# Strassen products that accumulate onto a PSUM bank of an earlier product

## The chip, the cores and the metric

The kernel runs on one core of one Trainium2 chip. The metric is the device time of one execution in microseconds (us); three runs of the kernel before gave 1822.58, 1822.8 and 1824.99 us, median 1822.8.

## The reference

One layer of a Griffin-style block on x (1024 tokens, 1024 channels), float32 in and out. Cut to what matters here:

```
mod = silu(c) @ ada_w + ada_b                # sh1, sc1, g1, sh2, sc2, g2
h = rmsnorm(x, ln1_g) * (1 + sc1) + sh1
q, k, v, cb, cc, cx, ga, gb = split(h @ w_in)
y_a = stick_breaking_attention(norm(q), norm(k), v)
y_b = cb * causal_dwconv(cc * cx, conv_w)
merged = sigmoid(ga) * (y_a @ w_branch_a) + sigmoid(gb) * (y_b @ w_branch_b)
x = x + g1 * (merged @ w_out)
h = rmsnorm(x, ln2_g) * (1 + sc2) + sh2
f = (silu(h @ w_ffn_gate) * (h @ w_ffn_up)) @ w_ffn_down
x = x + g2 * f
```

The FFN has 2816 hidden channels. Two stages are touched: the columns of `w_in` that give cb, cc, cx, ga and gb (called the gates below), and the FFN's gate and up projections.

## The kernel before, in words

A float32 matrix is held as a high part (float32r) and a low part, and a product of two matrices is three matmuls: high with high, high with low, low with high. TensorE (PE) works on 128x512 tiles; a product of the two-level scheme below takes 12 matmuls (`half_prod`, L126 to L133: four slices of the contraction, three matmuls each, on lines L131, L132 and L133). Weights come by DMA as `raw` (SyncE's queue), ScalarE (ACT) makes the high part `whi`, VectorE (DVE) the low part `wlo`.

The gates and the FFN's gate and up projections use Strassen's scheme in Winograd's form. A block computes four 128x512 outputs, c11, c12, c21, c22, from seven products P1 to P7 (the factor in the code counts from 0, so P6 is factor 5). The weight sums S1 to S4 are made by GpSimd (POOL) from the raw halves, in `ws` tiles; the sums of the activations (the factors `ft`, `rh`/`rl`, `big`) exist already. There are 20 such blocks in the gates (`for g, (sec, j) in enumerate(gates)`, L730) and 22 in the FFN (`strassen(j, e, ...)`, j from 0 to 10, e = 0 for gate, 1 for up). With every product in a PSUM bank of its own, a block ends in one copy on ScalarE and seven sums on VectorE (helper `tt`, L136):

```
c11 = P1 + P2
c21 = P1 + P6;  c12 = c21 + P5;  c22 = c12 + P7
c21 = c21 + P7;  c21 = c21 + P4;  c12 = c12 + P3
```

The gates have six banks (`pj`), the FFN eight (`e`).

What follows a block: in the gates a sigmoid (L749) and a store issued on ScalarE's queue (L750), or the short convolution (L721 to L724). Between the blocks stands other work: `mods_later`, which makes the later modulation vectors from `ada_w`. It loads 512 KB pieces (`ad<-ada`, `uu<-ada`, issued on ScalarE's queue, L639), takes a dot on VectorE over 128x1024 elements (L640), turns the sums by two transposes (`tr`), copies them (`uu`, L655) and stores a vector (`d_g<-uu`, L656). In the FFN a Silu (L1453) or a product with the gate side follows, then the seven operands that the down projection needs of the hidden values (four of them sums, on POOL, for the first and last j on VectorE), each split and stored by `put_f` (ScalarE L1445, VectorE L1446 through L136, store L1447). c11 of the gate side lives in the tile `wt(0)`, which these hidden sums read.

The start of the FFN is written out by hand: while the last token tiles of x are normalised (`tail_tr`, `tail_ev`, transposes L1206), the activation's quarters `h2b` are combined and split by `split_big` (ScalarE L1199 into `rh` and `big`, VectorE into `rl`), and the first products P1 and P2 of (0, gate), (0, up), (1, gate) and (1, up) are made ahead into `pre` and `pq`.

The order within an engine is set by a tile scheduler that walks the program with its own cost table; every engine then works its list strictly in order, and waits at semaphores for others. An instruction that waits therefore holds all that stand behind it in its engine's list, DMA issues on ScalarE's and SyncE's lists included.

Of the kernel before, what the change touches and what calls it, by code (L numbers as in the profile page):

```python
# [12 lines left out]
ALU = mybir.AluOpType  # L13
# [17 lines left out]
def block_kernel(tc, x, x_t, cols, ada_1, ada_2, ada_row, w_q, w_kv, w_cg, w_a, w_b, w_o, w_g, w_u, w_d, out):  # L31
# [91 lines left out]
        nc.gpsimd.tensor_tensor(out=r, in0=m[:, :w], in1=nhalf[:, :w], op=ALU.pow)  # L123
        return r

    def half_prod(ps, w, fh, fl):  # L126

        wh = w[0].rearrange("p (k m) -> p k m", k=4)
        wl = w[1].rearrange("p (k m) -> p k m", k=4)
        for k in range(4):  # L130
            nc.tensor.matmul(ps, wh[:, k, :], fh[:, k, :], start=(k == 0), stop=False)  # L131
            nc.tensor.matmul(ps, wh[:, k, :], fl[:, k, :], start=False, stop=False)  # L132
            nc.tensor.matmul(ps, wl[:, k, :], fh[:, k, :], start=False, stop=(k == 3))  # L133

    def tt(eng, out, a, b, op):
        eng.tensor_tensor(out=out, in0=a, in1=b, op=op)  # L136
# [375 lines left out]
    def g_split(src):  # L512
        split_at.append(split_at.pop(0))
        hi, lo = (split_at[0].tile([P, 512], F32R, tag=t_, bufs=GS if split_at[0] is gw else GS2, name=nm(t_))
                  for t_ in ("whi", "wlo"))
        nc.scalar.activation(hi, src, AF.Copy)
        tt(nc.vector, lo, src, hi.bitcast(F32), ALU.subtract)
        return hi, lo
# [75 lines left out]
    def g_prod(w, q):  # L594
        ps = g_bank()
        half_prod(ps, w, *fac[q])
        return ps
# [132 lines left out]
    for g, (sec, j) in enumerate(gates):  # L730
        raw, raw2 = raws
        p1, p2 = pre[g] if g in pre else (g_prod(g_split(raw[:, :512]), 0), g_prod(g_split(raw[:, 512:]), 1))
        a11, a12, a21, a22 = raw[:, :512], raw[:, 512:], raw2[:, :512], raw2[:, 512:]
        s1, s2_, s3, s4 = (gp2.tile([P, 512], F32, tag=f"ws{q}", bufs=1, name=nm("ws")) for q in range(4))
        with tc.high_priority() if g == 0 else ExitStack():
            tt(nc.gpsimd, s3, a11, a21, ALU.subtract)
            tt(nc.gpsimd, s2_, a22, s3, ALU.subtract)
            w6 = g_split(s2_)
        tt(nc.gpsimd, s1, a21, a22, ALU.add)
        ws4 = nc.gpsimd.tensor_tensor(out=s4, in0=a12, in1=s2_, op=ALU.subtract)  # L740
        if g + 1 < len(gates):
            raws = two_raw(g + 1)
        c11, c21, c12, c22 = (gp.tile([P, 512], F32, tag=f"c{q}", bufs=2, name=nm("c")) for q in range(4))

        def put(c, m, n):
            if sec == 5:
                pend.append((c, m, n))
            elif sec > 2:
                nc.scalar.activation(c, c, AF.Sigmoid)  # L749
                nc.scalar.dma_start((d_sga, d_sgb)[sec - 3][m, :, n * 512:(n + 1) * 512], c)  # L750
            elif sec == 1:
                ccs[m, n] = c
            elif n == 1 and m >= 4:
                ccs["late"] = c
            else:
                put_u(c, m, n)
                if n == 0 and m >= 4:
                    put_u(ccs["late"], m, 1)

        def later():  # L760
            if len(pmm) > 1 or pmm and not pend:
                sum_q(*pmm.pop(0))
            if pend:
                put_q(*pend.pop(0))
            elif g > 3 and not pmm:
                with tc.issue_after(ws4.ins):
                    next(eq, None)

        nc.scalar.activation(c11, p1, AF.Copy)
# [462 lines left out]
    NJ = NH // 2  # L1232
    pq = {}

    def prod(ps, w, q):
        half_prod(ps, w, rh[q], rl[q])

    def product(w, q):
        ps = bank()
# [137 lines left out]
    tt(nc.vector, x1p, pq[6], x1p, ALU.add)  # L1377
# [27 lines left out]
    def strassen(j, e, src, done=lambda q, c: None):  # L1405

        c21, c12, c22 = (ct(f"c{q}{e}", 1) for q in range(1, 4))
        if (j, e) == (0, 0):
            tt(nc.vector, c12, pq[5], x1p, ALU.add)
            p4 = product(sp5, 3)  # L1410
            tt(nc.vector, c22, pq[7], c12, ALU.add)
            tt(nc.vector, c21, pq[7], x1p, ALU.add)
            tt(nc.vector, c12, pq[3], c12, ALU.add)
            tt(nc.vector, c21, p4, c21, ALU.add)
            return x11, c12, c21, c22
        p1, p2, s1, s2, s3, s4, a22 = wsum(j, e, src, nc.gpsimd)
        if (j, e) == (0, 1):
            c11, c1 = x21, x2p
        else:
            c11, c1 = ct("c01", 1) if e else wt(0), c21  # L1420
            nc.scalar.activation(c21, p1, AF.Copy)  # L1421
# [5 lines left out]
        p5 = product(split(s1), 4)  # L1427
        tt(nc.vector, c12, p5, c21, ALU.add)
        p7 = product(split(s3), 6)
        tt(nc.vector, c22, p7, c12, ALU.add)  # L1430
        done(3, c22)
        tt(nc.vector, c21, p7, c21, ALU.add)
        p3 = product(split(s4), 2)
        tt(nc.vector, c12, p3, c12, ALU.add)
        done(1, c12)
        p4 = product(split(a22), 3)
        tt(nc.vector, c21, p4, c21, ALU.add)
        done(2, c21)
        return c11, c12, c21, c22

# [252 lines left out]
```

## Time and profile before

| | |
|---|---|
| median of 3 runs | 1822.8 us (1822.58 to 1824.99) |
| the profiled execution, its span | 1822.9 us |
| PE busy | 1794.7 us, 98% |
| VectorE busy | 1362.9 us, 75% |
| ScalarE busy | 809.6 us, 44% |
| GpSimd busy | 367.4 us, 20% |
| chain that ended last | PE 83%, VectorE 8%, DMA 5%, ScalarE 1% |

The kernel before stands for 1822.8 us; the trace shows one execution, whose span of 1822.9 us is that time. A matmul's row lasts 0.39 us, but matmuls overlap, so time on PE is counted from start to start. A row of the view of waits reads: engine, the output and line that waited, what released it, then the total in us, how often, and the longest. In square brackets a row of the timeline shows the idle time ahead of it and what ended it.

### The profile page before, as it was taken

What the parts mean: (1) busy time and instruction counts of PE and PEld (TensorE: products, weight loads), DVE (VectorE), ACT (ScalarE), POOL (GpSimd) and SP (SyncE); (2) the same over time, 40 slices, a digit from 0 to 9 for tenths busy, and PEclk for the clock granted to TensorE, in tenths of its full rate; (3) what the DMA queues carried; (4) which work ended last, traced back from release to release, by engine and by line L of the source; (5) the groups of instructions that cost most, each with busy time, mean ns of one, the idle gap of its engine ahead of it and who ended that gap; (6) DMA issues with size and microseconds to landing.
All of it is one profiled execution on the core that took longest, in us unless ns stands there. A gap on an engine that the chain in (4) does not pass through costs nothing.

```text
span 1822.9 us, 24550 instructions
## 1 busy us (share of the span) xinstructions
PE 1794.7 (98%) x8629; PEld 1492.0 (82%) x8629; DVE 1362.9 (75%) x1980; ACT 809.6 (44%) x1510; POOL 367.4 (20%) x277
## 2 busy tenths in 40 slices
PE   8999999999999899999999999999999999999999
PEld 6888877888778788888888888877888888878887
DVE  5876586778894699999997554699877878644776
ACT  5534363333433466666675221764444344322321
POOL 0024234632232000000000000115434444200000
PEclk9999999999999999999999999999999999999999
DMA  9479644223684977696654546424443444299876
GB/s 381 162 247 386 235 163 141 81 98 125 230 287 155 265 203 185 191 336 172 160 135 153 184 155 204 129 91 183 164 150 139 150 169 155 107 347 346 274 230 220
DMA packets 165102, 359.57 MB, mean 197 GB/s; under 512 B 15522, under 2 KB 60906, under 8 KB 163828
## 3 DMA queue, kind: packets, MB, share of 16 engines
q1 hardware_dynamic: 128300, 289.65, 48.6%
q10 hardware_dynamic: 35672, 64.68, 9.9%
q0 software_dynamic: 1008, 3.67, 0.5%
q8 instruction: 69, 1.13, 0.3%
q14 instruction: 53, 0.43, 0.1%
HBM read 247.32 MB, written 110.66 MB: 196 GB/s over the span
## 4 chain that ended last, share of the span: by engine, by line
PE 83%; DVE 8%; DMA 5%; issue 2%; ACT 1%; POOL 0%; SPq 0%; ACTq 0%; DVEq 0%; POOLq 0%
PE e L131 7%; PE e L133 7%; PE e L132 7%; PE pj L293 7%; PE pj L131 5%; PE pj L133 5%; PE pj L132 5%; PE pj L995 4%; PE pj L997 4%; PE pj L996 4%; PE e L1521 4%; PE e L1523 4%; PE e L1522 4%; PE tr L919 3%; PE o L935 2%
## 5 line engine op out<-in xcount | busy, mean ns | idle before, releaser
L905 DVE TENSOR_TENSOR_SCAN pt<-pt,mk 128x128 f32<-128x128 f32 (+7 forms) x128 | 172.6, 1348 | 3.2 <-ACT pt L897 3.2
L131 PE MATMUL e<-big,whi 128*128 128x512 f32 x352 | 138.2, 393 | 3.8 <-ACT c L1421 3.8
L132 PE MATMUL e<-big,whi 128*128 128x512 f32 x352 | 137.9, 392 | 0.0
L133 PE MATMUL e<-big,wlo 128*128 128x512 f32 x352 | 137.8, 392 | 0.0
L293 PE MATMUL pj<-whi,big 128*128 128x512 f32 x448 | 133.7, 396 | 3.1 <-ACT big L262 3.1
L136 DVE TENSOR_TENSOR c<-e,c 128x512 f32<-128x512 f32 x138 | 92.9, 687 | 54.8 <-PE e L133 53.8
L131 PE MATMUL pj<-big,whi 128*128 128x512 f32 x320 | 125.3, 392 | 1.6 <-DVE c L136 1.6
L133 PE MATMUL pj<-big,wlo 128*128 128x512 f32 x320 | 124.9, 390 | 0.0
L132 PE MATMUL pj<-big,whi 128*128 128x512 f32 x320 | 124.6, 389 | 0.0
L122 POOL TENSOR_SCALAR rs_m<-ss 128x1 f32<-128x1 f32 x8 | 1.7, 218 | 607.5 <-ACT xn L1324 607.5
L1521 PE MATMUL e<-whi,f 128*128 128x512 f32 (+1 forms) x319 | 121.8, 382 | 0.9 <-ACT whi L1182 0.6
L1522 PE MATMUL e<-wlo,f 128*128 128x512 f32 (+1 forms) x319 | 121.8, 382 | 0.0
L1523 PE MATMUL e<-whi,f 128*128 128x512 f32 (+1 forms) x319 | 121.6, 382 | 0.0
L136 DVE TENSOR_TENSOR c<-pj,c 128x512 f32<-128x512 f32 x140 | 93.1, 682 | 36.0 <-PE pj L133 35.2
L897 ACT ACTIVATE pt<-z,rq 128x512 f32<-128x512 f32 (+1 forms) x192 | 105.1, 576 | 25.4 <-PE z L896 25.0
L995 PE MATMUL pj<-big,whi 128*128 128x512 f32 x256 | 113.9, 445 | 0.0
L136 POOL TENSOR_TENSOR ws<-raw,raw 128x512 f32<-128x512 f32 x40 | 54.1, 1354 | 278.3 <-DMA raw<-w_cg 130.0
L923 DVE TENSOR_TENSOR atl<-tr,ath 128x512 fp32r<-128x512 f32 (+1 forms) x192 | 103.1, 550 | 9.2 <-ACT ath L922 7.2
L922 ACT ACTIVATE ath<-tr 128x512 fp32r<-128x512 f32 (+1 forms) x192 | 93.2, 488 | 33.1 <-PE tr L919 32.2
L132 PE MATMUL e<-rl,whi 128*128 128x512 f32 x264 | 102.8, 390 | 1.5 <-DVE rl L136 1.5
L133 PE MATMUL e<-rh,wlo 128*128 128x512 f32 x264 | 102.7, 389 | 0.0
L131 PE MATMUL e<-rh,whi 128*128 128x512 f32 x264 | 102.7, 389 | 0.0
(269 smaller groups left out, 4863.2 us busy)
## 6 DMA issues: line engine op xcount, KB each, us to landing
f<-d_f SPq DMA_DIRECT2D x77, 512.0 KB, 4.3
d_f<-fs SPq DMA_DIRECT2D x70, 512.0 KB, 3.2
raw<-w_cg SPq DMA_DIRECT2D x40, 512.0 KB, 3.2
raw<-w_u SPq DMA_DIRECT2D x26, 512.0 KB, 3.3
raw<-w_g SPq DMA_DIRECT2D x25, 512.0 KB, 3.6
raw<-w_kv SPq DMA_DIRECT2D x20, 512.0 KB, 4.0
ad<-ada ACTq DMA_DIRECT2D x19, 512.0 KB, 4.5
ld<-ada SPq DMA_DIRECT2D x16, 512.0 KB, 4.3
```

The lines of the kernel that those rows point to most:

```text
L131: nc.tensor.matmul(ps, wh[:, k, :], fh[:, k, :], start=(k == 0), stop=False)
L132: nc.tensor.matmul(ps, wh[:, k, :], fl[:, k, :], start=False, stop=False)
L133: nc.tensor.matmul(ps, wl[:, k, :], fh[:, k, :], start=False, stop=(k == 3))
L136: eng.tensor_tensor(out=out, in0=a, in1=b, op=op)
L293: nc.tensor.matmul(ps, a, b, start=(k == 0 and q == 0), stop=(k == KT - 1 and q == 2))
L897: nc.scalar.activation(pt[:, off + s0:off + s0 + m], z[:, :m], AF.Sigmoid, scale=rq[:, 1, i, h:h + 1])
L905: nc.vector.tensor_tensor_scan(out=pt[:, rev], data0=pt[:, rev], data1=mk[:, rev], initial=1.0, op0=ALU.mult, op1=ALU.max)
L923: nc.vector.tensor_tensor(out=tl[:, :nb, c0:c0 + P], in0=src, in1=th[:, :nb, c0:c0 + P].bitcast(F32), op=ALU.subtract)
L995: nc.tensor.matmul(ps, wh, rh_, start=(k == 0), stop=False)
L1521: nc.tensor.matmul(o, sh, w[0][:, c], start=(j == 0), stop=False)
L1522: nc.tensor.matmul(o, sh, w[1][:, c], start=False, stop=False)
L1523: nc.tensor.matmul(o, sl, w[0][:, c], start=False, stop=(j == NJ - 1))
```

## The change

In a block, P6 and then P5 are accumulated onto P1's bank, and P4 onto P7's bank, by matmuls whose first one does not clear the bank. ScalarE copies P1's bank three times: as c11 (P1), after P6 as c21 (P1+P6), after P5 as c12 (P1+P6+P5). VectorE is left with four sums: c11 + P2, c12 + P7 (into c22), c12 + P3, and c21 + P7, which by then holds P7+P4. P6 may start when c11's copy has read the bank, P5 when c21's has, P4 when c22's sum has read P7's bank. In the gates' first block P4 keeps a bank of its own. At the FFN's start the up side's P6 and P5 are interleaved with the gate side's, and its P7 is made there too.

```diff
-    def half_prod(ps, w, fh, fl):
+    def half_prod(ps, w, fh, fl, onto=False):
...
-            nc.tensor.matmul(ps, wh[:, k, :], fh[:, k, :], start=(k == 0), stop=False)
+            nc.tensor.matmul(ps, wh[:, k, :], fh[:, k, :], start=(k == 0 and not onto), stop=False, skip_group_check=onto)
...
+        def onto(ps, src, q):
+            half_prod(ps, src if isinstance(src, tuple) else g_split(src), *fac[q], onto=True)
+
         nc.scalar.activation(c11, p1, AF.Copy)
-        p4 = g_prod(g_split(a22), 3) if g + 1 == len(gates) else None
-        p6 = g_prod(w6, 5)
-        tt(nc.vector, c21, p6, c11, ALU.add)
+        onto(p1, w6, 5)
         tt(nc.vector, c11, p2, c11, ALU.add)
         put(c11, j, 0)
         later()
-        p5 = g_prod(g_split(s1), 4)
-        tt(nc.vector, c12, p5, c21, ALU.add)
-        p3 = g_prod(g_split(s4), 2) if g == 0 else None
-        p7 = g_prod(g_split(s3), 6)
+        p7, p3 = (None, g_prod(g_split(s4), 2)) if g == 0 else (g_prod(g_split(s3), 6), None)
+        nc.scalar.activation(c21, p1, AF.Copy)
+        onto(p1, s1, 4)
+        nc.scalar.activation(c12, p1, AF.Copy)
+        p7 = p7 or g_prod(g_split(s3), 6)
         tt(nc.vector, c22, p7, c12, ALU.add)
         put(c22, j + 4, 1)
         later()
-        tt(nc.vector, c21, p7, c21, ALU.add)
         p3 = p3 or g_prod(g_split(s4), 2)
         tt(nc.vector, c12, p3, c12, ALU.add)
         put(c12, j, 1)
         later()
-        p4 = p4 or g_prod(g_split(a22), 3)
-        tt(nc.vector, c21, p4, c21, ALU.add)
+        if g:
+            onto(p7, a22, 3)
+        else:
+            tt(nc.vector, c21, p7, c21, ALU.add)
+            p7 = g_prod(g_split(a22), 3)
+        tt(nc.vector, c21, p7, c21, ALU.add)
...
-    pq[6] = product(sp2, 5)
-    pq[5] = product(sp1, 4)
-    pq[3] = product(sp3, 2)
+    up2 = split(ws1[1])
+    prod(pq[1], sp2, 5, True)
+    prod(pre[0, 1][0], up2, 5, True)
+    nc.scalar.activation(x1p, pq[1], AF.Copy)
+    up1 = split(ws1[0])
+    prod(pq[1], sp1, 4, True)
+    nc.scalar.activation(x2p, pre[0, 1][0], AF.Copy)
+    x14 = wsb(0)
+    nc.scalar.activation(x14, pq[1], AF.Copy)
...
     split_big(rh[6], rl[6], h2b[0][0])
+    pq[3] = product(sp3, 2)
+    prod(pre[0, 1][0], up1, 4, True)
     pq[7] = product(sp4, 6)
...
         if (j, e) == (0, 1):
-            c11, c1 = x21, x2p
+            c11, c21, p1, p7 = x21, x2p, pre[0, 1][0], pq["up"]
         else:
-            c11, c1 = ct("c01", 1) if e else wt(0), c21
+            c11 = ct("c01", 1) if e else wt(0)
+            nc.scalar.activation(c11, p1, AF.Copy)
+            prod(p1, split(s2), 5, True)
+            tt(nc.vector, c11, p2, c11, ALU.add)
+            p7 = product(split(s3), 6)
             nc.scalar.activation(c21, p1, AF.Copy)
-            tt(nc.vector, c11, p2, c21, ALU.add)
-        p6 = bank()
-        prod(p6, split(s2), 5)
-        tt(nc.vector, c21, p6, c1, ALU.add)
+            prod(p1, split(s1), 4, True)
+        nc.scalar.activation(c12, p1, AF.Copy)
```

The lists of PE keep their number of matmuls; VectorE's goes from 1947 to 1822 rows, ScalarE's from 1610 to 1694. Lines below L770 stand some 5 to 10 lines further down in the new kernel. Three places of ScalarE's list follow.

In the gates, ScalarE's list from the store of the first later modulation vector (`d_g0`) on; L639 are loads of `ada_w` pieces, L769 is the copy of a block's P1. Before:

```order
L656 DMA d_g0_80<-uu_824_4307 128x1024
L639 DMA ad_904_4665<-ada_2 128x1024
L516 ACTIVATE whi_872_4519<-raw_844_4380 128x512
L639 DMA ad_937_4822<-ada_2 128x1024
L769 ACTIVATE c_846_4384<-pj_834_4338 128x512
L639 DMA ad_939_4827<-ada_2 128x1024
L639 DMA uu_863_4485<-ada_2 128x1024
```

The same place in the new list; L772 is the copy of P1 (c11), L780 the copy that gives c12:

```order
L656 DMA d_g0_80<-uu_780_4249 128x1024
L639 DMA ad_854_4599<-ada_2 128x1024
L639 DMA ad_884_4752<-ada_2 128x1024
L639 DMA ad_886_4757<-ada_2 128x1024
L780 ACTIVATE c_768_4154<-pj_754_4106 128x512
L516 ACTIVATE whi_806_4346<-ws_796_4312 128x512
L639 DMA uu_816_4423<-ada_2 128x1024
L772 ACTIVATE c_802_4326<-pj_790_4280 128x512
```

The load `uu_816` waits for the store of `d_g0`; a copy of P1 now stands right behind it, where before the next copy of P1 stood ahead of the loads of `uu`.

At the FFN's start, ScalarE's list around the split of the activation sums (`rh6` and `rh3`, L1199). Before:

```order
L1199 ACTIVATE big_2374_11682<-h2b11_11069 128x1024 x2
L1369 ACTIVATE wt_2380_11756<-e_2355_11612 128x512
L1199 ACTIVATE big_2374_11682<-h2b01_11068 128x1024 x2
L1199 ACTIVATE rh6_11684<-h2b00_11070 128x1024 x2
L1182 ACTIVATE whi_2387_11825<-raw_2386_11823 128x512
L1182 ACTIVATE whi_2400_11951<-ws_2208_10753 128x512
```

The same place in the new list, where `split_big` is L1204; L1380, L1383 and L1385 are the copies of the two P1 banks after P6 and after P5:

```order
L1374 ACTIVATE wt_2321_11678<-e_2296_11534 128x512
L1204 ACTIVATE big_2315_11604<-h2b01_10990 128x1024 x2
L1187 ACTIVATE whi_2323_11686<-ws_2149_10675 128x512
L1380 ACTIVATE wt_2302_11568<-e_2276_11452 128x512
L1187 ACTIVATE whi_2325_11715<-ws_2148_10674 128x512
L1383 ACTIVATE wt_2321_11678<-e_2296_11534 128x512
L1385 ACTIVATE ws_2327_11732<-e_2276_11452 128x512
L1204 ACTIVATE rh6_11606<-h2b00_10992 128x1024 x2
```

Three copies of accumulated banks and two splits now stand ahead of `rh6`.

In the middle of the FFN, ScalarE's list where a block's copy of P1 follows the copies `fs` of the hidden sums of the block before. Before:

```order
L1445 ACTIVATE fs_2689_13291<-wt_2685_13278 128x512
L1445 ACTIVATE fs_2693_13314<-c10_2624_12995 128x512
L1445 ACTIVATE fs_2694_13319<-wt_2686_13279 128x512
L1182 ACTIVATE whi_2746_13545<-ws_2737_13511 128x512
L1421 ACTIVATE c10_2695_13323<-e_2703_13336 128x512
```

The same place in the new list:

```order
L1187 ACTIVATE whi_2651_13400<-ws_2647_13391 128x512
L1454 ACTIVATE fs_2602_13175<-wt_2598_13162 128x512
L1454 ACTIVATE fs_2605_13197<-c10_2542_12886 128x512
L1432 ACTIVATE wt_2622_13255<-e_2615_13219 128x512
L1187 ACTIVATE whi_2653_13417<-ws_2648_13392 128x512
```

The copy of P1 goes into the tile `wt` instead of a tile of c21, and P6 of the same block is in PE's list behind it, 43 matmuls after P1's last.

More of the change, by code (lines that the diff above doesn't have):

```diff
@@ L130, in half_prod @@
         for k in range(4):
-            nc.tensor.matmul(ps, wh[:, k, :], fh[:, k, :], start=(k == 0), stop=False)
-            nc.tensor.matmul(ps, wh[:, k, :], fl[:, k, :], start=False, stop=False)
-            nc.tensor.matmul(ps, wl[:, k, :], fh[:, k, :], start=False, stop=(k == 3))
+            nc.tensor.matmul(ps, wh[:, k, :], fh[:, k, :], start=(k == 0 and not onto), stop=False, skip_group_check=onto)
+            nc.tensor.matmul(ps, wh[:, k, :], fl[:, k, :], start=False, stop=False, skip_group_check=onto)
+            nc.tensor.matmul(ps, wl[:, k, :], fh[:, k, :], start=False, stop=(k == 3), skip_group_check=onto)
     def tt(eng, out, a, b, op):
@@ L1408, in strassen @@
         if (j, e) == (0, 0):
-            tt(nc.vector, c12, pq[5], x1p, ALU.add)
-            p4 = product(sp5, 3)
-            tt(nc.vector, c22, pq[7], c12, ALU.add)
+            tt(nc.vector, c22, pq[7], x14, ALU.add)
+            tt(nc.vector, c12, pq[3], x14, ALU.add)
+            pq["up"] = product(split(ws1[2]), 6)
+            prod(pq[7], sp5, 3, True)
             tt(nc.vector, c21, pq[7], x1p, ALU.add)
-            tt(nc.vector, c12, pq[3], c12, ALU.add)
-            tt(nc.vector, c21, p4, c21, ALU.add)
             return x11, c12, c21, c22
```

15 lines of the change are left out of this document (5 added, 10 removed).

## The prediction

> **What bounds the kernel now.** I read the page's busy shares first, then the waits of TensorE, then windows of 20 us over the two touched stages (gates about 190 to 590 us, FFN gate/up about 1190 to 1590 us), then the timeline at each lost stretch.
>
> ```profile
> PE 1794.7 (98%) x8629; PEld 1492.0 (82%) x8629; DVE 1362.9 (75%) x1980; ACT 809.6 (44%) x1510; POOL 367.4 (20%) x277
> PE e L131 <- ACT c L1421: 3.8, 1, 3.8
> PE pj L133 <- DVE wlo L136: 2.0, 1, 2.0
> PE pj L131 <- DVE c L136: 1.6, 3, 0.7
> PE e L132 <- DVE rl L136: 1.5, 1, 1.5
> ```
>
> PE is the bound. The other engines matter only through these four waits, the only ones over 1 us in the touched stages. In the windows (columns: us; PE, PEld, DVE, ACT, POOL busy with counts; clock; DMA) I count matmuls:
>
> ```profile
> 440.00:460.00 20.00, 19.29 (x85) 15.69 (x84) 19.17 (x24) 6.10 (x10) 7.60 (x4) 1.00 0.71 260
> 460.00:480.00 20.00, 19.11 (x83) 15.17 (x82) 20.00 (x32) 7.21 (x13) 7.38 (x4) 1.00 0.77 275
> 540.00:560.00 20.00, 18.04 (x72) 14.76 (x73) 14.28 (x23) 9.71 (x18) 5.62 (x5) 0.91 0.50 157
> 1200.00:1220.00 20.00, 18.53 (x82) 15.03 (x81) 20.00 (x25) 12.28 (x17) 0.00 (x0) 1.00 0.16 52
> 1220.00:1240.00 20.00, 20.00 (x90) 16.57 (x89) 17.50 (x23) 7.97 (x15) 11.49 (x8) 1.00 0.46 154
> 1240.00:1260.00 20.00, 16.21 (x62) 12.85 (x61) 19.97 (x27) 9.28 (x17) 8.78 (x5) 0.83 0.57 217
> ...
> 1236.23 0.39 PE L131 MATMUL e<-rh,whi 128*128 128x512 f32 x1
> 1238.95 0.39 PE L131 MATMUL e<-rh,whi 128*128 128x512 f32 x1
> ```
>
> An undisturbed window holds 90 (1220 to 1240). The two starts at the end are 12 matmuls apart: 2.72 us a product, 0.2267 us a matmul. Missing matmuls then price the losses: 440 to 480: 12, 2.7 us; 540 to 560: 18, 4.1 us; 1200 to 1220: 8, 1.8 us; 1240 to 1260: 28, 6.3 us. So the gates lose 6.8 us and FFN's start 8.1 us. Elsewhere in the two stages PE runs without a gap, so 14.9 us (0.8%) is all that the change could win. How the losses arise:
>
> ```profile
> 538.98 2.31 DVE L640 CUSTOM_DVE_ANT_0 uu<-uu,cab 128x1024 f32<-128x1024 f32 x1
> 541.96 0.50 PE L133 MATMUL pj<-ft,wlo 128*128 128x512 f32 x1 [1.99 <-DVE wlo L136]
> 1214.56 0.50 PE L132 MATMUL e<-rl,whi 128*128 128x512 f32 x1 [1.47 <-DVE rl L136]
> 1250.41 0.60 ACT L1421 ACTIVATE c<-e 128x512 f32<-128x512 f32 x1 [2.35 <-DVE fs L136]
> 1251.06 0.79 PE L131 MATMUL e<-big,whi 128*128 128x512 f32 x1 [3.79 <-ACT c L1421]
> ```
>
> In the gates a split part (wlo) stands on VectorE behind a modulation dot (L640). In the FFN the last split of h2 is late, and later a product wants a bank whose copy stands on ScalarE behind f sums. After the waits of 1.99 and 3.79 us the clock falls (0.91, 0.83): of the 4.1 and 6.3 us, 2.1 and 2.5 are slow clock. After 1.47 us only 0.3 is lost beside the wait.
>
> **The change, part by part.**
>
> ```profile
> L136 DVE TENSOR_TENSOR c<-e,c 128x512 f32<-128x512 f32 x138 | 92.9, 687 | 54.8 <-PE e L133 53.8
> L136 DVE TENSOR_TENSOR c<-pj,c 128x512 f32<-128x512 f32 x140 | 93.1, 682 | 36.0 <-PE pj L133 35.2
> L769 ACT ACTIVATE c<-pj 128x512 f32<-128x512 f32 x20 | 11.7, 583 | 3.0 <-DVE msum L640 2.1 <-DMA raw<-w_cg 0.9
> L1421 ACT ACTIVATE c<-e 128x512 f32<-128x512 f32 x20 | 11.6, 581 | 3.7 <-DVE fs L136 2.3 <-PE e L133 1.4
> ```
>
> *Sums and copies.* 125 VectorE rows go, about 0.69 us each: 85 us of work. 84 ScalarE copies come, 0.58 us each: 49 us. TensorE keeps its products. VectorE and ScalarE lie beside PE, so neither figure enters the sum; only what becomes of the lost stretches does.
>
> *New waits.* A product that accumulates must wait until the copy (or the c22 sum) has read its bank. In the order, 24 or more matmuls (5.4 us) lie between almost everywhere, other products filling them, against 0.58 us for the copy. Exceptions: in the gates' first block P5 follows P6 on one bank after a single matmul: copy plus two hand-overs, **0.8 us** lost. The FFN start has gaps of 10 to 14 matmuls, priced below.
>
> *Gates, where the dots run (440 to 500 us).*
>
> ```profile
> L640 DVE CUSTOM_DVE_ANT_0 ad<-ad,cab 128x1024 f32<-128x1024 f32 x19 | 28.9, 1546 | 0.0
> 452.64 1.21 DVE L640 CUSTOM_DVE_ANT_0 uu<-uu,cab 128x1024 f32<-128x1024 f32 x1
> 453.90 0.33 ACTq L639 DMA_DIRECT2D uu<-ada  x1
> d_g<-uu ACTq DMA_DIRECT2D x2, 512.0 KB, 5.6
> ACT whi L516 <- DMA d_g<-uu: 3.3, 1, 3.3
> ```
>
> A dot takes 1.2 us alone, 2.3 beside POOL (538.98); a DMA issue holds ScalarE's queue 0.35. I followed both engines' order with these durations. With three sums fewer per block wlo keeps ahead: I find no wait at the place of the 1.99 us, so its 4.1 us go. Two new ones come on ScalarE, where a DMA issue that waits holds everything behind it. At 456.6 us a c11 copy stands behind an issue waiting for a dot (VectorE's fourth dot ends at 451.1, three splits at 0.6 and that dot follow, 454.1), then a c12 copy, a split and three more issues (454.5 + 0.6 + 0.6 + 1.2), itself 0.6: ready at 457.5, **1.0 us** late. At 496 us the c11 copy stands behind an issue that waits for d_g0: issued 2.7 us after the last modulation transpose (three splits, two copies), landing 5.6 later, then issue and copy, 9.3; PE is there after 39 matmuls, 8.8: **0.6 us**. Of the small waits (2.7 us lost at 440 to 480, 1.6 of it listed) I keep half of the unlisted, **0.6 us**. Gates: 6.8 before, 3.0 after: **3.8 us gained**. Ends: only the 0.8 remains (6.0 gained); or the d_g0 wait grows to 2.0 us with 2.1 of slow clock and the rest stays (7.8 after, 1.0 lost).
>
> *FFN start.*
>
> ```profile
> 1190.83 0.48 PE L131 MATMUL e<-big,whi 128*128 128x512 f32 x1
> 1204.72 2.20 ACT L1199 ACTIVATE rh<-h2b 128x1024 fp32r<-128x1024 f32 x2 [3.10 <-DVE h2b L136]
> 1206.34 2.35 DVE L136 TENSOR_TENSOR rl<-h2b,rh 128x1024 fp32r<-128x1024 f32 x2
> 1212.68 1.28 ACT L1453 ACT_TABLE_LOAD   x1
> 1216.76 0.68 DVE L136 TENSOR_TENSOR ws<-raw,ws 128x512 f32<-128x512 f32 x1
> 1217.36 0.68 DVE L136 TENSOR_TENSOR c<-e,c 128x512 f32<-128x512 f32 x1
> 1220.83 1.38 POOL L136 TENSOR_TENSOR ws<-raw,raw 128x512 f32<-128x512 f32 x1 [36.10 <-DMA raw<-w_g]
> 1224.73 2.20 ACT L1182 ACTIVATE whi<-ws 128x512 fp32r<-128x512 f32 x4 [2.42 <-POOL ws L136]
> 1229.43 1.29 POOL L136 TENSOR_TENSOR ws<-raw,raw 128x512 f32<-128x512 f32 x1 [3.35 <-DMA raw<-w_u]
> 1234.15 1.68 ACT L1182 ACTIVATE whi<-ws 128x512 fp32r<-128x512 f32 x3 [0.46 <-POOL ws L136]
> ```
>
> Count from 1190.8, the first product after h2's last transposes. In the new order ScalarE's split rh6 stands behind the copy of P1+P6+P5, whose last matmul is the 84th: 1209.9. So rh6 starts at 1210.5, not 1204.7. PE needs it after 108 matmuls, at 1215.3, so the 1.47 us wait goes. But what follows is 5.8 us later too: after rh6 VectorE, whose rows follow 0.6 apart, has 2.35 (rl6, from 1211.7), 0.6, 2.35 (h2b), 0.6, 2.35 (rl3), then 0.6 each. The c sum that frees P7's bank ends at 1221.4, PE wants it after 132 matmuls at 1220.7: **0.7 us**. A wlo is late by **0.6**. The S sum (1216.8 before) ends at 1222.6; its raw load, POOL and ScalarE follow as before (1217.4 to 1224.7 to the second split), so the split is ready at 1231.1 where PE stands at 1230.2 after 168 matmuls: **1.0**, with its wlo **0.2** more. The next load leaves when POOL's fourth sum ends (1231.3) and takes 3.3; from POOL's start to the first split 4.7 passed before (1229.4 to 1234.2), 0.6 the split: 1239.9. PE wants it after 192 matmuls, with the waits so far (2.5) at 1236.9, where before this product came three places later: **3.1 us** with the hand-over, and then slow clock **2.1**. The 3.79 us wait goes: that bank's next product now comes behind all this. FFN start: 8.1 before, 7.7 after: **0.4 us gained**. Ends: POOL sums at 1.3 each (the last wait 2.3) and no slow clock, 4.8 after (3.3 gained); at 1.7 each (1.2 more ahead of that load, 0.5 behind it), slow clock 2.5, 9.8 after (1.7 lost).
>
> The trace shows the clock falling after 1.99 us, so I charge it for 3.1. The Trainium skill, "TensorE: Matmul & The Clock Gate", section "What's actually happening", puts the fall after at least one idle window of about 3.4 us; by that the 1.99 us wait should have cost nothing more, and this trace disagrees. By its rule the 2.1 would fall away and the sum would be 1816.6.
>
> *Sum.* 3.8 + 0.4 = 4.2 us off the profiled span, 1822.9, which lies 0.1 from the median of the runs, 1822.8: **1818.7 us**.
>
> **The rivals.**
>
> *More is won (1816).* The 3.1 us wait is under 2.5, as POOL runs beside a quieter VectorE, and the clock stays: FFN wins 2 to 3, the gates 4 to 5. For: VectorE loses 85 us. Against: its queue at FFN's start waits for ScalarE, not for its own load.
>
> *Nothing is won (1822.5).* ScalarE's new copies wait behind DMA issues at more places in the gates, as its 3.3 us wait for d_g shows, and eat the 3.8; the FFN's 0.4 is left. Against: only two places came out of my walk.
>
> *Slower (1829), in FFN's steady part.* c11 of the gate side lives in a tile that the f sums of the block before still read, and now P6 waits for that copy; before it had a bank of its own.
>
> ```profile
> 1376.21 0.69 DVE L136 TENSOR_TENSOR c<-e,c 128x512 f32<-128x512 f32 x1 [0.23 <-PE e L133]
> 1384.85 1.73 POOL L136 TENSOR_TENSOR wt<-wt,c 128x512 f32<-128x512 f32 x1
> 1388.72 0.58 ACT L1421 ACTIVATE c<-e 128x512 f32<-128x512 f32 x1
> ```
>
> From P4's end (1376.1) through four POOL sums to the copy's end (1389.3) pass 13.2 us; in the new order 67 matmuls, 15.2 us, lie between P4's end and P6 (75 in every other block). Once the chain is over 15.2, about 0.5 us more on each POOL sum, each of nine blocks stalls: at 1 us, 9 us, less what is won, 1829. Against: 2.0 us of slack, and less VectorE work to slow POOL.
> The Trainium skill, "PSUM — Partial Sum Buffer", section "Summary: rules for kernel authors", advises reading PSUM while matmuls run from a different bank than theirs; this change gives that up, and the 3.79 us wait for a copy is what the trace has of its price.
>
> **How the numbers follow.** Forecast 0.45, more won 0.20, nothing won 0.20, slower 0.15. About 0.2% (3.6 us) is what a measurement can tell from no change, and the forecast lies on that edge: a little over half of its case counts as faster. Faster 0.20 + 0.25 = 0.45; within 0.20 + 0.18 = 0.38; slower 0.17. The ends of both parts together give 1813.6 to 1825.6; the range goes to 1827 to take in a part of the slower case: 1814 to 1827.
>
> **What would show it.** Right: no wait of PE for wlo near 540 us, none for rl; a wait of 2.5 to 4 us for whi in FFN's start, on a POOL sum behind a raw load, with the clock falling after it. Wrong: waits of PE for ScalarE's copies (the new lines in the gates or the FFN) that recur block after block; or FFN's start without a wait over 2 us.

## The result and the profile after

| | before | after |
|---|---|---|
| median | 1823.89 us (1822.58 to 1826.0, 4 runs) | 1837.03 us (1835.71 to 1841.61, 4 runs) |
| span of the profiled execution | 1822.9 us | 1833.9 us |

The ratio is 1.0073, with an interval of 1.0058 to 1.0089: the changed kernel is slower by 13 us (0.7%). The prediction said 1818.7 us, 1814 to 1827, and that is wrong in sign and outside its range.

The page of the changed kernel, its first part, and below it the view of TensorE's waits:

```profile
PE 1796.4 (98%) x8629; PEld 1491.6 (81%) x8629; DVE 1308.9 (71%) x1855; ACT 847.0 (46%) x1594; POOL 375.2 (20%) x277
```

```profile
PE z L900 <- DMA skh<-d_k: 7.2, 1, 7.2
PE e L131 <- ACT whi L1187: 5.4, 2, 3.9
PE pj L131 <- DVE c L136: 2.5, 2, 1.8
...
PE tr L686 <- ACT gt L678: 1.2, 1, 1.2
...
PE pj L133 <- DVE wlo L136: 1.0, 2, 0.5
...
PE e L133 <- DVE wlo L1188: 0.8, 2, 0.6
...
PE pj L131 <- ACT c L772: 0.6, 1, 0.6
```

The rows moved as counted (125 and 84), but VectorE is only 54 us less busy where the prediction has 85, and ScalarE 37 us more where it has 49; neither figure is in its sum. Three of the four waits that the prediction priced are gone (the copy's 3.8, wlo's 2.0, rl's 1.5). At the top stands a wait that it never names: `z`, the first product of the attention, for its key tile `skh`. Windows of 20 us, of the changed kernel and then of the kernel before (columns as before: PE, PEld, DVE, ACT, POOL busy with counts, clock, DMA):

```profile
540.00:560.00 20.00, 19.98 (x93) 16.40 (x92) 12.78 (x18) 9.38 (x17) 5.93 (x4) 1.00 0.36 129
...
580.00:600.00 20.00, 18.18 (x84) 14.86 (x84) 5.13 (x8) 6.43 (x11) 0.00 (x0) 1.00 0.31 118
600.00:620.00 20.00, 12.17 (x60) 9.72 (x59) 2.79 (x5) 2.00 (x4) 0.00 (x0) 0.85 0.96 296
1200.00:1220.00 20.00, 20.00 (x92) 16.59 (x90) 15.12 (x21) 11.14 (x20) 0.00 (x0) 1.00 0.08 26
1220.00:1240.00 20.00, 19.03 (x82) 14.80 (x80) 17.29 (x22) 12.00 (x18) 4.82 (x3) 1.00 0.38 132
1240.00:1260.00 20.00, 14.22 (x52) 10.44 (x53) 18.52 (x24) 10.58 (x20) 9.97 (x7) 0.91 0.49 166
```

```profile
580.00:600.00 20.00, 20.00 (x98) 16.85 (x97) 6.45 (x10) 5.22 (x9) 0.00 (x0) 1.00 0.60 207
600.00:620.00 20.00, 16.34 (x78) 13.03 (x77) 6.88 (x12) 5.98 (x14) 0.00 (x0) 0.91 1.14 265
```

At 540 to 560 there are 93 matmuls in place of 72: that wait and its slow clock are gone, 4.8 us won at 0.2267 us a matmul. At 580 to 620 there are 144 in place of 176: 7.3 us lost. After the wait of 7.2 us the clock is 0.85. From 1200 to 1260 there are 226 in place of 234: 1.8 us lost. These counts take short transposes (0.11 us) for whole matmuls, so they are rough; the shifts below are not touched by that.

To add this up I follow one matmul, by its place in TensorE's order, through both timelines and take the difference of its two starts; where the two orders hold short transposes at different places, their own time is taken out. The table gives how this shift grows. Gates is the gates up to near the end of their last block, hand-over from there to the end of the attention (within which, its first 10 us apart, it moves by 0.8 us at most), FFN start the first two blocks of the FFN. All traces measured are in it.

| kernel | gates | hand-over | FFN start |
|---|---|---|---|
| changed kernel | +0.6 | +7.8 | +1.7 |
| e1, P4 of the last gates block early | +0.3 | +2.9 | +2.2 |
| e2, before, that P4 late | +0.3 | +5.0 | -0.6 |
| e4, gates as before | +0.9 | +0.2 | +1.7 |
| e5, the same, rh6 first | -1.5 | +0.7 | +4.4 |
| e7, last gates block as before | +1.7 | +2.7 | +1.9 |
| e8, the same, FFN as before | +2.8 | +4.2 | -2.7 |
| e9, the same, FFN's block 0 as before | +2.8 | +2.8 | -0.8 |
| e11, as e9, first four gates blocks too | +1.5 | +3.8 | +0.9 |
| e12, last two gates blocks and FFN as before | +1.4 | +2.5 | -2.4 |
| e13, reload on GpSimd's queue | +1.0 | +9.5 | +1.9 |
| e14, three gates blocks accumulate, FFN as before | -3.7 | -0.7 | -0.5 |
| e15, changed kernel, no reload | +1.1 | +6.8 | +2.8 |
| e16, before, no reload | +1.8 | +0.3 | -0.9 |

In the changed kernel the rest of its 11.0 us is 0.9 ahead of the gates, where the code is the same. The column of the gates shows how far one trace can be trusted: the kernels whose gates are as before up to the last block's P4 (e2, e4, e5, e16) lie between -1.5 and +1.8 there.

### The profile page after: what moved, and what is told of

Its sections match the earlier page's. It is cut to its first block, busy times and chain, and to the rows that moved or that the text cites. A ratio compares the mean times of both kernels' runs of the same rounds, so it can differ in the third digit from the quotient of the medians.

```text
span 1833.9 us, 24377 instructions
## 1 busy us (share of the span) xinstructions
PE 1796.4 (98%) x8629; PEld 1491.6 (81%) x8629; DVE 1308.9 (71%) x1855; ACT 847.0 (46%) x1594; POOL 375.2 (20%) x277
## 4 chain that ended last, share of the span: by engine, by line
PE 86%; DVE 6%; DMA 4%; issue 1%; ACT 1%; POOL 1%; ACTq 0%; SPq 0%; DVEq 0%; POOLq 0%
PE pj L293 9%; PE e L133 7%; PE e L131 7%; PE e L132 7%; PE pj L131 5%; PE pj L133 5%; PE pj L132 5%; PE pj L1000 4%; PE pj L1001 4%; PE pj L1002 4%; PE e L1530 4%; PE e L1531 4%; PE e L1532 4%; PE tr L924 3%; PE o L940 2%; PE z L900 2%
## 5 line engine op out<-in xcount | busy, mean ns | idle before, releaser
L136 POOL TENSOR_TENSOR ws<-raw,raw 128x512 f32<-128x512 f32 x40 | 59.5, 1486 | 328.8 <-DMA raw<-w_cg 124.6
L1188 DVE TENSOR_TENSOR wlo<-ws,whi 128x512 fp32r<-128x512 f32 x84 | 72.5, 873 | 44.7 <-ACT whi L1187 40.1
L136 DVE TENSOR_TENSOR wlo<-raw,whi 128x512 fp32r<-128x512 f32 x108 | 79.7, 740 | 33.2 <-ACT whi L516 33.0
L293 PEld LDWEIGHTS pj<-whi,big 128*128 128x128 f32 x448 | 85.1, 191 | 21.8 <-ACT big L262 4.2
```

The source lines that it names most:

```text
L293: nc.tensor.matmul(ps, a, b, start=(k == 0 and q == 0), stop=(k == KT - 1 and q == 2))
```

## Where the 7.8 us arise

In the last gates block the order on TensorE was P1, P2, P4, P6, P5, P7, P3; now it is P1, P2, P6, P7, P3, P5, P4, with P6, P5, P4 accumulated. The end of this block in the changed kernel's timeline, rows of all engines in order of time; 600.11 is the last matmul of the gates:

```profile
595.47 0.63 ACT L516 ACTIVATE whi<-raw 128x512 fp32r<-128x512 f32 x1 [6.14 <-PE pj L132]
596.01 0.58 ACT L780 ACTIVATE c<-pj 128x512 f32<-128x512 f32 x1
596.74 1.41 DVE L136 TENSOR_TENSOR c<-pj,c 128x512 f32<-128x512 f32 x2
597.48 0.50 PE L131 MATMUL pj<-big,whi 128*128 128x512 f32 x1 [1.82 <-DVE c L136]
600.11 0.39 PE L133 MATMUL pj<-big,wlo 128*128 128x512 f32 x1
600.30 0.80 SPq L1079 DMA_DIRECT2D big<-d_h  x2
600.53 0.69 DVE L136 TENSOR_TENSOR c<-pj,c 128x512 f32<-128x512 f32 x1 [2.38 <-PE pj L133]
601.26 0.63 ACT L749 ACTIVATE c<-c 128x512 f32<-128x512 f32 x1 [0.32 <-DVE c L136]
601.92 0.33 ACTq L750 DMA_DIRECT2D d_sga<-c  x1
605.08 0.65 SPq L832 DMA_DIRECT2D skh<-d_k  x1
610.66 0.57 SPq L833 DMA_DIRECT2D skl<-d_k  x1
...
612.34 0.60 SPq L832 DMA_DIRECT2D skh<-d_k  x1
618.95 0.44 PE L900 MATMUL z<-skh,sqt 128*128 128x128 f32 x1 [7.22 <-DMA skh<-d_k]
```

The same hand-over in the kernel before:

```profile
584.02 0.80 SPq L1074 DMA_DIRECT2D big<-d_h  x2
594.71 0.39 PE L133 MATMUL pj<-big,wlo 128*128 128x512 f32 x1
594.93 1.95 PE L653 MATMUL tr<-dm,msum 128*128 128x128 f32 x16
596.52 0.33 ACTq L750 DMA_DIRECT2D d_sga<-c  x1
599.77 1.24 SPq L827 DMA_DIRECT2D skh<-d_k  x1
601.07 0.74 SPq L828 DMA_DIRECT2D skl<-d_k  x1
603.12 0.57 SPq L827 DMA_DIRECT2D skh<-d_k  x1
609.63 0.30 PE L895 MATMUL z<-skh,sqt 128*128 128x128 f32 x1 [1.27 <-DMA skh<-d_k]
```

The reader sees a chain without cover. P5 ends; the copy of P1's bank (596.01) stands behind a split; VectorE's c22 sum reads P7's bank; only then may P4 start, 1.82 us late, as no next block has products to put between. P4 is also the last reader of `big`, into which 2 MB (`d_h`) are reloaded: issued at 600.3 where it was 584.0. Then c21's sum, sigmoid and store, 601.92 where the last store was 596.52. SyncE issues skl's load, a part of the attention's keys, only when that store has landed. The key tiles are loaded in two halves, and skh's second half stands behind this load in SyncE's list: it leaves at 612.34 where it left at 603.12, and z starts 6.6 us after it (6.5 before). Two views carry the last step, SyncE's waits and the DMA view of 590 to 625 us of the changed kernel (KB each, median us from issue to landing):

```profile
SPq L833 <- DMA d_sga<-c: 4.9, 1, 4.9
```

```profile
big<-d_h SPq DMA_DIRECT2D x2, 1024.0 KB
...
d_sga<-c ACTq DMA_DIRECT2D x3, 256.0 KB, 8.7
...
cy<-d_y SPq DMA_DIRECT2D x1, 256.0 KB, 10.7
```

Before, a cy load took this long in the same stretch:

```profile
cy<-d_y SPq DMA_DIRECT2D x4, 256.0 KB, 6.6
```

## The experiments

Theory A was at first that P4's late place alone makes the keys late, because SyncE's list stands at the reload until P4 has ended. Rivals were the block's tail, the FFN, and a cost spread over all blocks. Numbers are medians with the kernel before on the same chip beside them, ratios with their intervals.

**e1: P4 of the last gates block early again, in its own bank.**

```diff
+        p4 = g_prod(g_split(a22), 3) if g + 1 == len(gates) else None
         onto(p1, w6, 5)
...
-        if g:
+        if g and p4 is None:
             onto(p7, a22, 3)
...
-            p7 = g_prod(g_split(a22), 3)
+            p7 = p4 or g_prod(g_split(a22), 3)
```

> The changed kernel, but the gates' last block makes P4 first and in a bank of its own, as the kernel before did (one VectorE sum more there). Theory A: the 7.2 us wait of the first attention product comes from SyncE's list: the reload of two activation tiles (big from d_h) waits for P4, the last reader of them, and the attention's key loads (skh) stand behind it. Then the reload leaves near 586 us instead of 600, the wait for skh falls under 2 us and the kernel is 7 to 8 us faster than the changed kernel: about 1829. Rival B: the wait comes from the accumulated banks being held longer at the end of the gates (the 1.8 us wait for a c sum ahead of it) or from DMA traffic, and P4's place does not matter: the wait stays at 6 to 8 us and the time at 1835 to 1838.

Measured: 1830.5 beside 1825.3, ratio 1.0033 (1.0021 to 1.0045). The wait for skh fell only to 4.5 us, the hand-over from 7.8 to 2.9. SyncE's waits in 590 to 622 us, and the landing of the stores in its DMA view:

```profile
SPq L834 <- DMA d_sga<-c: 6.0, 1, 6.0
```

```profile
d_sga<-c ACTq DMA_DIRECT2D x3, 256.0 KB, 5.4
```

So P4's place is worth 4.9 us in the trace (by medians, each over the kernel before beside it, 7.9: 13.1 against 5.2, with wide intervals), and another 2.9 stay: now P5 is last, and its copy, the sums that need it, three sigmoids and three stores come after it.

**e2: the kernel before, with that P4 at the block's end, in its own bank.**

```diff
-        p4 = g_prod(g_split(a22), 3) if g + 1 == len(gates) else None
+        p4 = None
```

> The kernel before, but the gates' last block makes P4 last like every other block; nothing else is changed and every product keeps a bank of its own. Theory A: about 7 to 8 us slower than the kernel before, 1831 to 1832, with a wait for skh of 6 to 8 us. Rival B: no change, 1823 to 1824, wait for skh 1 to 2 us.

Measured: 1827.71 beside 1825.3, ratio 1.0014 (1.0004 to 1.0024); the wait for skh is 6.4 us, the hand-over +5.0. Without any accumulation the late place alone costs 5.0 us in this trace and 2.4 by medians (0.7 to 4.4 by the interval), both less than the 7 to 8 expected. That the 5.0 is so near e1's 4.9 is in part chance: no wait for a bank is in it, while the changed kernel has one that e1 has not (split up behind e15).

**e4: gates as before, FFN as changed**, and **e5: the same, with the h2b difference and rh6's split written ahead of the accumulated products** (a try at the FFN's new waits).

> The kernel before with the FFN's part of the change alone; the gates are as before. Start-to-start times in the two traces give the FFN's start 1.7 us to the bad. If the parts add up: 1.7 us slower than the kernel before, 1825 to 1826, with the 3.9 us wait for whi in the FFN's start and no new wait behind it. Rival: the FFN's waits were carried over from the gates; then faster than before by 2 us or more.

> The same with the difference for rh6 and the split of rh6 written ahead of the FFN's first accumulated products and their copies, so that ScalarE makes rh6 before it waits for P1+P6 and P1+P6+P5. Theory C, from the prediction: rh6 behind those copies puts VectorE's chain, the raw loads and POOL some 5 us back, and this makes the waits of the FFN's start; then they all but go and the kernel is 5 to 7 us faster than the FFN part alone: about 1819, faster than the kernel before. Rival D: the order of the raw loads and POOL's sums alone sets the 3.9 us wait, since the products come three places earlier: it stays over 3 us and the time within 2 us of the FFN part alone.

Measured: e4 1827.61, ratio 1.0013 (1.0002 to 1.0024): the FFN has about 2.4 us of the loss, +1.7 in the trace, with the same wait of 3.9 us for whi. e5 1831.69, ratio 1.0032 (1.0021 to 1.0043): slower, not faster. In e5's timeline two waits stand where none was, and the long one is still there:

```profile
1206.99 0.50 PE L131 MATMUL e<-big,whi 128*128 128x512 f32 x1 [2.77 <-ACT whi L1182]
1208.33 0.80 PE L133 MATMUL e<-big,wlo 128*128 128x512 f32 x1 [0.61 <-DVE wlo L1183]
...
1244.06 0.80 PE L131 MATMUL e<-big,whi 128*128 128x512 f32 x1 [3.75 <-ACT whi L1182]
```

rh6 waits for VectorE ahead of a split that TensorE needs sooner. That rh6's place behind the copy makes the long wait is not borne out by this edit: in e5 other splits still stand behind the copies. The FFN start as built stays unmended here.

**e7, e8, e9, e11: the last gates block as before; in e8 also the FFN; in e9 only its block 0; in e11, on top of e9, also the first four gates blocks.** The edit in e7 (e11: `g < 4 or g + 1 == len(gates)`):

```diff
+        if g + 1 == len(gates):
+            nc.scalar.activation(c11, p1, AF.Copy)
+            p4 = g_prod(g_split(a22), 3) if g + 1 == len(gates) else None
+            p6 = g_prod(w6, 5)
...
+        else:
+            nc.scalar.activation(c11, p1, AF.Copy)
+            onto(p1, w6, 5)
...
```

> The changed kernel with its last gates block computed as before (P4 first, each product in its own bank, P3 last); all other gates blocks and the FFN as changed. Theory A (the whole shift between gates and attention comes from that block: 4.9 us because P4, made last, keeps the activation tiles and holds SyncE's queue, the other 2.9 because the block then ends on P5, whose copy and three sums and stores come after, and skl's load stands behind the store of c): both go, 7.8 us less than the changed kernel, which is 13.1 over before: 5 us over before, ratio 1.003; skh wait of PE under 2 us; the boundary shift within 0.5 us of before. Rival B (only P4's place matters and the rest is contention of the new copies in the blocks ahead): like the run with P4 early alone, 5 over before by medians there, with skh wait 4.5 us and a boundary shift of 2.9 us. The medians can hardly tell these (2.9 us), the boundary in the trace does.

> The same gates as in the run beside it, with the FFN as before. Left is the gates part without its last block. Theory A: gates net 0.3 to 0.6 us slower than before, nothing at the boundary, nothing in the FFN: before plus 0.5 us, ratio 1.000 (0.999 to 1.001). Rival B: before plus 3.5, ratio 1.002.

> As the run beside it, and in the FFN the products of hidden blocks 1 and on accumulate as changed, while block 0 (both sides) is as before. Theory A: the steady part is neutral (its added copies lie beside PE), so the same as the run beside it, ratio 1.000; the FFN start's waits are those of before (1.5 and 3.8 us). The prediction's slower rival (POOL's f sums make c11's copy late block by block): 5 to 10 us more, ratio 1.003 to 1.006, with a wait of PE for an ACT copy in every gate block.

> As the run beside it, and the first four gates blocks (section 5) also as before. Theory A: the small waits of the first blocks (copy 0.45, tr on gt 1.2 us) go, some 2 us, while the wait of 2.0 us with its slow clock near 540 us stays away: 2 us faster than before, ratio 0.999 (0.998 to 1.000). Rival (the early losses are spread over all gates blocks by ScalarE's added copies): no better than the run beside it, ratio 1.000.

Measured, beside 1823.9: e7 1832.08, ratio 1.0044 (1.0030 to 1.0057); e8 1828.84, 1.0021 (1.0011 to 1.0031); e9 1832.05, 1.0039 (1.0026 to 1.0051); e11 1832.56, 1.0042 (1.0028 to 1.0056). Theory A missed on all but parts. The hand-over stays at +2.7 to +4.2 although the last block is as before: the theory that this block alone makes it falls. In TensorE's order fourteen of the sixteen short transposes (`tr`, L653) that stood behind the last block in the kernel before now stand ahead of its P4, which so ends some 1.8 us later, and its P3 1.6 us. e9 is above e8 by about 3 us with overlapping intervals; its FFN trace has one wait of 1.6 us for a copy (`wt`) that e8 has not, once and not block after block (4.5 us in e11, whose FFN is e9's). e11 does what was expected of the early blocks (from the gates' start to their seventh block its shift is 0.8 where e7 to e9 have 3.0 to 3.5), and is no faster for it: it loses again further on, with waits of 2.26 us for whi at 500.7 and 1.75 for the dots' sums at 542.8.

**e12: FFN as before, the last two gates blocks as before** (the condition of e8 is changed).

```diff
-        if g + 1 == len(gates):
+        if g + 2 >= len(gates):
```

> FFN as before; gates as changed but for the last two blocks, which are as before. It stands beside the earlier run that had only the last block as before, whose boundary between gates and attention still shifted by 3.8 us. There, the block before the last still accumulated, its late P4 was interleaved with the last block's P4, and the last block's P4 ended 8 matmuls later in the order, its P3 7 later; here 4 later each. Theory A (the hand-over has no slack: what comes later at the end of the gates comes later through SyncE's list of loads, place for place): the boundary shift falls with the places, to 1 to 2 us; SyncE's reload of the activation tiles is issued about 1 us later than before, counted from TensorE's own time, instead of 1.8. Rival (the shift is from anything that the accumulating blocks leave behind, whatever the order at the end): still 3 to 4 us. Time: before plus 2 to 3 us by A, plus 4 to 5 by the rival.

**e13: the changed kernel with the reload issued on GpSimd's queue.**

```diff
-                    nc.sync.dma_start((hh, hl)[e][1][:, :4].bitcast(F32), d_h[e])
+                    nc.gpsimd.dma_start((hh, hl)[e][1][:, :4].bitcast(F32), d_h[e])
```

> The changed kernel, with one edit: the two reloads of the activation tiles (d_h) go by GpSimd's queue, so that SyncE's list no longer waits for P4 of the last gates block; P4 itself stays last. Theory A (the wait of SyncE for P4 is what makes the key loads late): the last raw load and the loads behind it leave about 1 us or more earlier, skh's issue at 601 to 604 in place of 605.1, as it also waited for the reload's landing; the wait of PE for skh falls from 7.2 to 2 to 5 us; 2 to 5 us faster than the changed kernel, 8 to 11 over before, ratio 1.004 to 1.006. What is left is the last split of a raw tile and the store of the last c, on which skl's load waits. Rival (only the block's tail, the copies, sums and stores after P4, makes the key loads late, and SyncE's wait for P4 is covered by it): no change, ratio 1.007, skh wait about 7 us.

**e14: FFN as before, and only gates blocks 15 to 17 accumulate** (again e8's condition).

```diff
-        if g + 1 == len(gates):
+        if g not in (14, 15, 16):
```

> FFN as before; in the gates only three blocks (the 15th to 17th of 20) accumulate, all others are as before, so that the order at the end of the gates is that of before. The wait of 1.99 us for wlo stood in the 18th block, behind VectorE's sums and dots. Theory A: with nine sums fewer ahead of it that wait and its slow clock go (4 us), at a cost of at most 1 to 2 us of new small waits; no early loss, no shift at the boundary, FFN as before: 2 to 4 us faster than before, ratio 0.998 to 0.999. Rival (the added copies cost in the stage of the dots what the sums save): ratio 1.000 to 1.001.

Measured, beside 1825.21: e12 1828.23, ratio 1.0022 (1.0012 to 1.0032); e13 1836.99, 1.0070 (1.0057 to 1.0083); e14 1823.51, 0.9991 (0.9983 to 0.9999).

e13 refutes theory A's form: with SyncE no longer waiting for P4, skh is issued at 605.17 as before the edit, and TensorE's wait for it stays. Its own rows, SyncE's waits and TensorE's:

```profile
SPq L505 <- DVE wlo L136: 38.7, 4, 13.1
SPq L833 <- DMA d_sga<-c: 7.1, 1, 7.1
```

```profile
PE z L900 <- DMA skh<-d_k: 7.0, 1, 7.0
```

SyncE waits instead for the last split of a raw tile (a wait that the earlier stop at P4 had hidden), and then 7.1 us for the last store. What the reload costs cannot be its place in SyncE's list; its traffic was left, for e15 to test.

e12's hand-over is +2.5, between the two theories' numbers, so it decides nothing (eight of the sixteen transposes stand ahead there). e14 keeps the end of the gates word for word as before, and its hand-over is -0.7; the wait of 1.99 us near 540 us is gone:

```profile
540.00:560.00 20.00, 20.00 (x90) 16.54 (x89) 11.38 (x16) 8.63 (x14) 6.54 (x4) 1.00 0.40 142
```

The change thus does what it can where VectorE was late, with nine sums fewer; this version beats the kernel before by 0.1%, with an interval that all but touches 1.

**e15: the changed kernel without the reload of `d_h`. e16: the kernel before without it.** Both leave out 2 MB of loads.

```diff
-                for e in range(2):
-                    nc.sync.dma_start((hh, hl)[e][1][:, :4].bitcast(F32), d_h[e])
```

> The changed kernel without the two reloads of the activation tiles (2 MB of d_h, left out: the products that follow read what stood in the tiles before). Theory A2 (P4's late place makes the reload late, and its 2 MB of traffic then lie ahead of the last gates block's last store and of the key loads): the last store lands 4 to 6 us after its issue in place of 8.7, cy's load in 3 to 6 in place of 10.7; skl's issue comes at about 607 in place of 610.7; the wait of PE for skh falls from 7.2 to 2.5 to 4 us; the shift between gates and attention is 3 to 4.5 us in place of 7.8; time 3 to 5 us under the changed kernel, ratio 1.005. Rival (the tail alone: P4's bank wait, the last sum, its store; traffic costs nothing): skh wait 7 us, shift 7.5 to 8, ratio 1.007.

> The kernel before without the same two reloads (left out in the same way), as a control. Theory A2: its reload is landed before the key loads leave, so nothing goes but perhaps the small waits for skh and skl (1.3 and 0.8 us): 0 to 1.5 us faster, ratio 0.9995 to 1.000, boundary shift -1.5 to 0. Rival (any kernel wins some 4 us without 2 MB of loads at that place): ratio 0.998.

Measured, beside 1825.28: e15 1833.1, ratio 1.0046 (1.0031 to 1.0061); e16 1824.3, 0.9996 (0.9986 to 1.0007). SyncE's skl load of e15, the last matmul of the gates and TensorE's two waits of its timeline:

```profile
597.14 0.50 PE L131 MATMUL pj<-big,whi 128*128 128x512 f32 x1 [1.82 <-DVE c L136]
...
601.34 0.39 PE L133 MATMUL pj<-big,wlo 128*128 128x512 f32 x1
...
607.59 0.57 SPq L833 DMA_DIRECT2D skl<-d_k  x1
...
616.27 0.44 PE L900 MATMUL z<-skh,sqt 128*128 128x128 f32 x1 [3.07 <-issue]
```

skl leaves at 607.6 (expected 607) and the wait for skh is 3.1 us (2.5 to 4), the ratio 1.0046 (1.005); the control wins nothing that can be told from zero. So the late reload costs by its traffic, about 4 us by medians (1833.1 against 1836.99 and 1837.03). The hand-over in e15's trace, +6.8, is above the 3 to 4.5 expected: the wait of 1.82 us for P7's bank cost 3.7 us there from the matmul ahead of it to the first product behind P4 (13 steps of 0.2267 us taken off), against 2.1 in the changed kernel, as the clock fell to 0.94 in the window of 580 to 600 us (1.00 there in the changed kernel).

A count from the start of the last gates matmul to z leaves that wait out. It is 14.92 us before and 18.84 in the changed kernel, 19.12 in e13 and 14.93 in e15, and these last three run the same 57 operations on TensorE in it: the traffic of the late reload costs 3.9 us of the changed kernel's 7.8. (With the order of before e16 takes 15.12 and e2, with the reload late, 19.81.) Before, the same stretch also held sixteen short transposes of `mods_later` (594.93), 1.8 us of work that lay inside the wait for the keys. In the changed kernel all sixteen stand ahead of it, and TensorE waits that much longer instead. With the 2.1 us of P7's bank this makes 2.1 + 3.9 + 1.8 = 7.8.

That SyncE's reload delays ScalarE's store, and does so from GpSimd's queue as well (e13), agrees with the Trainium skill, "DMA: Bandwidth & Descriptors", section "Issuing engines are not separate DMA queues": transfers run on the same 16 DMA engines and interleave, whichever engine issued them. From the last store's issue to skl's pass 8.7 us in the changed kernel, 10.2 in e13 and 4.4 in e15.

## Why the prediction was wrong

The signs that the prediction named for being right all came: no wait for wlo near 540 us, none for rl, and a wait of 3.87 us for whi with a fallen clock. The loss lies where it named none.

*Failed: "In the order, 24 or more matmuls ... lie between almost everywhere ... Exceptions: in the gates' first block ... The FFN start".* The last gates block is an exception too, and the dear one. It has no next block to fill the gap, so P4 waits 1.82 us for the bank (the changed kernel, e13 and e15). And the diff drops the line that made P4 early in just this block; the prediction weighs P4 as an accumulated product, never as a moved one, with the reload that waits for its last read and the key loads behind. Measured: +7.8 us in the trace where the sum has nothing. Of these, 2.1 are P4's wait for P7's bank, gone with P4's early place (e1); 3.9 are the traffic of the late reload, gone without the reload (e15) and still there from another queue (e13); and 1.8 are the sixteen transposes that no longer fill the wait for the keys. The last part is read from the orders and not tested apart: the hand-over keeps 2.5 to 4.2 us in e7 to e9, e11 and e12, where fourteen or eight of them stand ahead, and nothing in e14, where all stand behind as before. e1 keeps 2.9 us with all sixteen ahead and P5 and three stores at the end; how its 2.9 divides is open.

*Mis-sized: gates, "6.8 before, 3.0 after".* The 4.1 us at 541.96 went as said (-4.0). The first block's 0.8 became 2.8 over the first six blocks: at 214.80 the copy (0.45 idle), at 240.13 a transpose behind ScalarE's `gt` (1.18), at 300.77 a c sum (0.68). In the stage of the dots the walk was right in kind: the copy that was to be late by 1.0 at 456.6 is late by 0.61 at 461.62, d_g0's 0.6 did not come, and 0.3 to 0.54 came at three other places; by shift this stage loses 1.7 more than before, which lost 2.7 there itself: 4.4 where 2.2 (1.0 + 0.6 + 0.6) were kept. Net gates: +0.6 in place of -3.8. (The bad end of 7.8 after does not follow from the terms that it names: 0.8, 1.0, 0.6, 2.0 and 2.1 make 6.5.)

*Right in kind, at the forecast's bad end: FFN start, "8.1 before, 7.7 after", with an end of 1.7 lost.* It lost 1.7. The wait on a c sum is 0.49 (0.7 said), whi 1.57 (1.0), wlo 0.58 (0.2), and the long one 3.87 (3.1). That size is in part chance: with the same FFN it is 3.9 in e4 and e15, but 2.3 to 2.5 in e1, e7 and e13. It has the cause that was named, in the changed kernel's timeline:

```profile
1238.25 3.15 POOL L136 TENSOR_TENSOR ws<-raw,ws 128x512 f32<-128x512 f32 x2
1241.43 0.33 SPq L1180 DMA_DIRECT2D raw<-w_u  x1
1244.79 1.31 POOL L136 TENSOR_TENSOR ws<-raw,raw 128x512 f32<-128x512 f32 x1 [3.39 <-DMA raw<-w_u]
1251.10 2.17 ACT L1187 ACTIVATE whi<-ws 128x512 fp32r<-128x512 f32 x4
1251.77 0.50 PE L131 MATMUL e<-big,whi 128*128 128x512 f32 x1 [3.87 <-ACT whi L1187]
```

The load leaves when POOL's fourth sum ends (1241.4) and takes 3.4; from there to the split pass 6.3 us, 4.7 were taken. The "before" side was mis-sized as well: of the six traces whose FFN is as before, the other five start it 0.5 to 2.7 us faster than the one that the prediction read, 1.2 on average over the six; those with the FFN as changed (the changed kernel, e1, e4, e7, e13 and e15) average +2.0. So the change costs about 3.2 us here.

*Refuted: the slower rival.* In FFN's steady part the shift doesn't move (11.0 at its start and its end). The 2.0 us of slack in c11's tile held. The sign of the result was not this rival's doing. The remark below it, that the change gives up reading one bank while matmuls run on another, misreads the change: the next product on a bank waits for the copy, and other products run on other banks meanwhile. Its price is that wait, 1.82 us in the last block.

*Sum.* Averages over the traces give about 1.1 us for the gates without their end (the changed kernel, e1, e7, e8, e9, e12, e13 and e15 against before, e2, e4, e5 and e16), 8.5 for the hand-over (the changed kernel and e13 against before, e4, e5, e14 and e16) and 3.2 for FFN's start: 12.8 us, beside 13.1 by medians.

## What to carry to other kernels

When an edit folds a special case into the general one (here the last block's early P4), price that case as a move: list the tiles of which the moved operation is the last reader, and the transfers and loads behind them. A chain of copy, accumulate, copy is free only while other products stand between its links; look at the last block of a loop, where none do. Apply such a change only where the engine that it relieves was late: three blocks of 20 gave a small gain (0.1%), all 42 a loss. And look at what fills a wait at a stage's end: work that moves ahead of it leaves the wait open.

## What the runs showed of the hardware

The same idle time of 1.82 us cost 2.1 us in one trace (granted clock 1.00 in 580 to 600 us) and 3.7 in another (0.94, e15). A wait of 1.99 us was followed by a clock of 0.91 in the kernel before (540 to 560 us), and one of 1.99 ahead of z in e14 by none below 1.00 (600 to 620 us). So the length of a wait of this size does not tell whether the clock falls. The Trainium skill, "TensorE: Matmul & The Clock Gate", section "What's actually happening", tells of a free-running window, so that the point of the change depends on where in it the first matmul lands; that agrees with these pairs, though its idle window of about 3.4 us is longer than the waits after which the clock fell here. And one trace is less sharp than its decimals: stages of identical code differed by up to 3.3 us between traces (-1.5 to +1.8 in the gates of e5 and e16).
